# A float32 encoder trunk on one core: the order of VectorE's work in the product blocks, and what is split at the end of a stage

## The chip, the core and the metric

The kernel runs on one core of a Trainium2 chip. The metric is the device time of one execution in microseconds, the median of several runs. TensorE (PE in the profile) multiplies, VectorE (DVE) and ScalarE (ACT) work on elements, GpSimd (POOL) issues some transfers, and SyncE's queue (SP) issues the others.

## The reference

The reference is a two-layer encoder on x of 256 tokens by 1024. Each layer is a feed-forward stage, a mixer and another feed-forward stage, each with a scaled residual and a layer norm behind it:

```python
def swiglu(x, w_in, w_out):
    gu = x @ w_in                              # 1024 x 5632
    g, u = gu[..., :D_FF], gu[..., D_FF:]      # D_FF = 2816
    return (jax.nn.silu(g) * u) @ w_out        # 2816 x 1024

def reference(x, ffn_w_in, ffn_w_out, ln_g, ln_b, ml_w_in, ..., at_w_out):
    for l in range(DEPTH):                     # 2
        x = layer_norm(ALPHA * x + 0.5 * swiglu(x, ffn_w_in[l, 0], ffn_w_out[l, 0]), ln_g[l, 0], ln_b[l, 0])
        y = mlstm_mixer(x, ...) if l == 0 else window_attention(x, ...)
        x = layer_norm(ALPHA * x + y, ln_g[l, 1], ln_b[l, 1])
        x = layer_norm(ALPHA * x + 0.5 * swiglu(x, ffn_w_in[l, 1], ffn_w_out[l, 1]), ln_g[l, 2], ln_b[l, 2])
    return x
```

The mixers are a bidirectional chunkwise mLSTM in layer 0 and a windowed attention with sinks in layer 1. Everything is float32.

## The kernel before

There are six stages: feed-forward, mLSTM, feed-forward, feed-forward, attention, feed-forward. To keep float32 accuracy, each operand of a matmul is split into a high and a low part: ScalarE writes the high part (`w_hi`, `h_hi`, `xT_hi`) and VectorE the difference as the low part (`w_lo`, `h_lo`, `xT_lo`). A product is then three matmuls (`mm3`): high by high, high by low, low by high.

**Weights.** All weights come from HBM as words of 128 partitions by 1024 values (512 KB). The class `Weights` (L155) holds the plan: a list of splits in a fixed order, each of one word. `load` issues a word's transfer on SP when a buffer is free (four for the tag `w_raw`; two for each of the tags `s_raw0` to `s_raw3`). `high` emits the ScalarE part of the next split, `low` the VectorE part, then drops the word's use and loads the next. Split words live in a ring of ten (`RING`). `take` gives the next words to a product, and forces the splits that are still missing; `done` says that words have been used.

**Seven products.** A feed-forward stage computes its first 768 columns of gate and up plainly. The other 2048 go in four blocks of 512 (`SEVENS`), each done by `seven` as a two-by-two block product with seven products in place of eight. Some of its weights are sums of words: VectorE adds one word to another (`tensor_add` in `sum`), or GpSimd issues a transfer that accumulates on top of a word already in SBUF. So the words `b11` of a block are split four times, at four states, and between two of these stands an addition or an accumulating transfer. `after` holds these additions by split, `needs` says which split has to come first. The plan's order differs from the order of use in one thing: the last two splits of a block (`late`) stand behind the first two of the next block; `turn` gives the order of use.

Inside a block the products are, in order, on the PSUM banks qa, qc, qb, qa, qa, qb, qa, with down-projections (`down`, twelve matmuls for each word of w_out) between them: three stand in the middle and one at the end of a full block, two in the last block. Behind each product an `end` function emits its element work on the tile `e` (names v["g0"], v["u0"], v["u1"], v["g1"]). `tr` turns a half of h = silu(g) * u by four TensorE transposes, and `split_evac` writes it as `h_hi` (ScalarE) and `h_lo` (VectorE). In a full block `tr` of v["u0"] stands behind the third down-projection, before the last product; `tr` of v["u1"] stands in the next block, behind its first product.

**The clocks.** While it writes the program, the class `Paced` keeps an estimate of each engine's time: `pe`, `vec`, `act` and `dma`, and of when each tile will be there (`when`, `mark`). In a feed-forward stage each matmul that is written calls `fill` (L278). It emits a split's high part if ScalarE's clock is less than 300 ns (`AHEAD`) ahead of TensorE's and the word is there 1000 ns (`SOON`) before; and, if VectorE's clock allows it, an addition or a low part under the same rule. All other VectorE work is written where its producer is written, and each engine runs its instructions in the written order. A transfer's landing is estimated as 2200 ns (`LANDING`) and 1340 ns (`LOADING`) behind TensorE's clock, that of an accumulating one as 8000 ns (`ADDING`).

**The end of a stage.** Behind the last block `fill` is switched off (`nc.filler = None`, L920), `load_ln` issues two transfers on SP for the layer norm's vectors (L921), and the last six words are taken. `W.done(0)` (L924) then splits as many of the next stage's words as the ring has room for, whether they have landed or not. `tail` (L612) does the last down-projections: first token half 0, both output halves, then token half 1. In between it runs the transposes of the last block (`between`), the residual and the layer norm (`Norm`, L569), and more calls of `W.done`, with numbers of splits from lists at the head of the file.

Of the kernel before, what the change touches and what calls it, by code (L numbers as in the profile page):

```python
# [45 lines left out]
SOON = -1000.0  # L46
LANDING = 2200.0
LOADING = 1340.0
SECOND = 1250.0
ADDING = 8000.0  # L50
# [98 lines left out]
class Weights:  # L149
# [5 lines left out]
    def __init__(self, nc, pool, words, plan, after, turns):  # L155
        self.nc, self.pool, self.words, self.plan, self.after = nc, pool, words, plan, after
        self.raw, self.parts, self.half, self.sums = {}, {}, [], []
        self.made = self.used = self.gone = 0
        self.room = 0
        self.order, self.left = turns, set(range(len(plan)))  # L160
        self.todo = {tag: [i for i, w in enumerate(words) if w["tag"] == tag] for tag in TAGS}
        self.free = {"v_raw": 0, **{tag: 0 for tag in TAGS}, "w_raw": RAW_BUFS}
        self.spool, self.send, self.vbufs = None, 0, 0
        self.uses = [0] * len(words)
# [49 lines left out]
    def split(self, upto):  # L214
        while self.made < min(upto, len(self.plan)):
            self.high()
        while self.half and self.half[0][0] < upto:
            self.low()

    def high(self):  # L220

        nc, i = self.nc, self.made
# [18 lines left out]
        self.made += 1  # L241
        return True

    def low(self):
# [15 lines left out]
        self.sums += [(i, *sum_) for sum_ in self.after.get(i, ())]  # L260
# [3 lines left out]
    def sum(self):  # L264
        nc = self.nc
        _, w, v = self.sums.pop(0)
        t = self.raw[w]
        if isinstance(v, int):
            nc.vector.tensor_add(t, t, self.raw[v])
            self.drop(v)  # L270
            self.load()
        else:
            nc.gpsimd.dma_start(t.rearrange("p (k f) -> p k f", k=self.words[w]["k"]), v, accum_op=OP.add)  # L273
            now = max(nc.vec, nc.pe)
            nc.dma = max(nc.dma, now + LANDING) + SHARE
            nc.mark(t, now + ADDING)

    def fill(self):  # L278

        nc = self.nc  # L280
        while True:
            act, vec = max(nc.act, nc.pe), max(nc.vec, nc.pe)
            if act < nc.pe + AHEAD and len(self.half) < 2 and self.made < min(self.room, len(self.plan)):
                p = self.plan[self.made]
                if (p["word"] in self.raw and nc.when(self.raw[p["word"]]) < act + SOON
                        and not any(p["needs"] == x for x in [h[0] for h in self.half] + [s_[0] for s_ in self.sums])):
                    self.high()
                    continue
            if vec < nc.pe + AHEAD:
                if self.sums and nc.when(*(self.raw[w] for w in self.sums[0][1:] if isinstance(w, int))) < vec + SOON:  # L290
                    self.sum()
                    continue
                if self.half and nc.when(self.half[0][1]) < vec + SOON:
                    self.low()
                    continue
            break

    def take(self, n):
        these = self.order[self.used:self.used + n]
        self.used += n  # L300
        self.split(max(these) + 1)
        return [self.parts[j] for j in these]
# [4 lines left out]
    def done(self, upto=None, most=None, high_only=False):  # L307
# [3 lines left out]
        while self.gone < upto:  # L311
            j = self.order[self.gone]
            self.left.discard(j)
            self.parts.pop(j, None)
            self.gone += 1
        self.room = max(self.room, min(self.left, default=len(self.plan)) + RING)
# [15 lines left out]
def trunk_kernel(ctx: ExitStack, tc: tile.TileContext, x, ffn_w_in, ffn_w_out, ln_g, ln_b, ml_w_in, ml_gate_b,  # L332
# [17 lines left out]
    def split_of(w, scale=None, needs=None):  # L350

        plan.append(dict(word=w, k=words[w]["k"], scale=scale, needs=needs, turn=len(plan)))
# [22 lines left out]
    def seven(w, c0, c1, n, down, late):  # L375
# [6 lines left out]
        first = len(plan)  # L382
        used = iter(range(99))

        def turn(n_):
            for p in plan[-n_:]:
                p["turn"] = first + 0.01 * next(used)

        s1 = [split_of(w_) for w_ in b11]
        turn(2)  # L390
        for j, a in enumerate(at(512, c1)):
            after[s1[j]] = [(b11[j], b12[j]), (b12[j], a)]
        late()
        for a in at(512, c0):
            piece(a, 2)
        turn(2)
        down()
        turn(1)
        s5 = [split_of(w_, None, p) for w_, p in zip(b11, s1)]
        turn(2)  # L400
        for j in range(2):
            after[s5[j]] = [(b11[j], b22[j])]
        full = n < SEVENS - 1
        s6 = [split_of(w_, None, p) for w_, p in zip(b11, s5)]
        turn(2)
        for j, a in enumerate(at(512, c0)):
            after[s6[j]] = [(b11[j], a)]
        down()
        turn(1)
        [split_of(w_, None, p) for w_, p in zip(b12, s1)]  # L410
        turn(2)
        for w_ in b22:
            split_of(w_)
        turn(2)
        if full:
            down()
            turn(1)
        at4 = [next(used) for _ in range(2)]
        if full:
            down()  # L420
            turn(1)

        def last():
            for j in range(2):
                split_of(b11[j], None, s6[j])
                plan[-1]["turn"] = first + 0.01 * at4[j]
        return last

    ends = {}
    for j, (kind, l, i, _) in enumerate(stages):  # L430
        if kind == "ffn":
# [13 lines left out]
            late = lambda: None  # L445
            for g in range(SEVENS):
                c0 = 768 + 512 * g
                late = seven(wi, c0, F + c0, g, lambda: down(1), late)
            late()
# [33 lines left out]
    W = Weights(nc, wpool, words, plan, after, [j for _, j in sorted((p['turn'], j) for j, p in enumerate(plan))])  # L483
# [52 lines left out]
    def split_evac(dst, src, scale=None, high=None):  # L536
        if scale is None:
            (high or nc.scalar.copy)(dst[0], src)
            nc.vector.tensor_sub(dst[1], src, dst[0].bitcast(F32))
# [20 lines left out]
    def load_ln(room, l, n):  # L560
        t = []
        for name, w in (("g", ln_g), ("b", ln_b)):
            a = room("ln_" + name)
            src = w[l, n]
            nc.sync.dma_start(a, bass.AP(tensor=src.tensor, offset=src.offset, ap=[[0, 128], [1, D]]))
# [46 lines left out]
    def tail(y, h, todo, first, norm, last, turn_at, between=None):  # L612
# [37 lines left out]
        W.done(most=TD[bound[0]])  # L650
        return lambda: emit_x(1, last)
# [5 lines left out]
    def ffn(l, i, n, pending, last):  # L657
        with ExitStack() as ph:
# [18 lines left out]
            def tr(hB, t, h):  # L677
# [3 lines left out]
                split_evac(pair(hB, A, A, tok(t)), p)  # L681
# [50 lines left out]
            def x_sum(name, a, op, b):  # L732
# [4 lines left out]
                split_evac(xs[name], f)  # L737
# [90 lines left out]

            def seven(full, before):
# [11 lines left out]
                def end2():  # L841
                    nc.vector.tensor_add(v["g0"], v["g0"], qc)
# [4 lines left out]
                def end6():  # L847
                    v["u0"] = copied(qa, "e2")
                    nc.scalar.activation(v["g0"], v["g0"], AF.Silu)

                def end3():
                    nc.vector.tensor_sub(v["u0"], qb, v["u0"])
                    nc.vector.tensor_mul(v["u0"], v["g0"], v["u0"])

                def end7():
                    nc.vector.tensor_sub(v["u1"], v["u1"], qa)
# [18 lines left out]
                if full:  # L875
                    down(1)
                    tr(hB, 0, v["u0"])
# [3 lines left out]
                return lambda: tr(hB, 1, v["u1"])  # L881
# [26 lines left out]
            def turn():  # L908
# [4 lines left out]
                split_evac(hp, p)  # L913
# [4 lines left out]
            if start:  # L918
                small_loads()
            nc.filler = None  # L920
            gb = load_ln(lambda name: pool.tile([128, D], F32, name=name, tag=TAGS[1], bufs=S_RAW), l, n)  # L921
# [552 lines left out]
```

## Time and profile before

| | |
|---|---|
| median of 3 runs | 948.33 us (946.0 to 948.74) |
| profiled execution, its own time | 948.53 us |
| its span, first to last instruction | 946.8 us |
| granted TensorE clock, mean over the span | 0.984 |
| TensorE busy | 918.3 us (97%) |
| VectorE busy | 810.6 us (86%) |
| ScalarE busy | 569.5 us (60%) |
| read from HBM | 206.65 MB, 219 GB/s over the span |

Nearly all compute instructions carry line L140, where a helper records each operation; so they are told apart by engine and tile: `pw` and `py` are PSUM banks (products, and down-projections or output projections), `w_hi` and `w_lo` the split weights, `s_raw` words of the blocks with sums, `w_raw` the other words, `e` the element work of a block. In a row such as `PE pw L140 <- DVE e L140: 7.7, 8, 2.3` the engine on the left waited for the one on the right, 7.7 us in all, 8 times, 2.3 us at most. In rows of the windows the columns are the stretch and its length, then for each engine the busy us and the number of instructions, the granted TensorE clock, the share of the DMA engines and GB/s. In a chain the columns are start, us and what.

### The profile page before, as it was taken

How to read it: one execution, taken by the hardware profiler on the slowest of the kernel's cores; microseconds unless marked ns; L12 is line 12 of the kernel's file. 1: busy time of each engine (PE TensorE's matmuls, PEld its weight loads, DVE VectorE, ACT ScalarE, POOL GpSimd, SP SyncE). 2: the span in 40 equal slices, each digit the busy share in tenths (PEclk: the TensorE clock that was granted, in tenths of full speed). 3: DMA queues.
4: the chain of work that ended last, by engine and by line, in shares of the span. 5: the costliest groups of instructions: out<-in, count | busy, mean ns of one | idle time of the engine just before them, and what ended most of it. 6: DMA issues, size and time to landing. Idle time of an engine off the chain costs nothing.

```text
span 946.8 us, 12553 instructions
## 1 busy us (share of the span) xinstructions
PE 918.3 (97%) x4459; PEld 763.5 (81%) x4459; DVE 810.6 (86%) x969; ACT 569.5 (60%) x793; POOL 155.5 (16%) x194
## 2 busy tenths in 40 slices
PE   9998999999999999999989999997999999999997
PEld 7786887889988888788878878886888888788885
DVE  5798998897699789999787999987868887989986
ACT  5575674645764566775535766764459564676670
POOL 0011122022321011211011111210345301212110
PEclk9998999999999999999989999999999999999999
DMA  8988997754625979987649799867343379889951
GB/s 283 354 202 272 275 283 165 239 173 151 225 95 178 335 186 321 252 251 204 218 146 356 178 278 310 252 156 235 121 156 120 104 246 287 233 224 274 290 135 45
DMA packets 100703, 208.53 MB, mean 220 GB/s; under 512 B 6904, under 2 KB 21264, under 8 KB 100640
## 3 DMA queue, kind: packets, MB, share of 16 engines
q1 hardware_dynamic: 82368, 173.04, 52.0%
q0 software_dynamic: 17696, 33.65, 20.6%
q10 hardware_dynamic: 576, 1.05, 0.3%
q8 instruction: 35, 0.57, 0.3%
q14 instruction: 28, 0.23, 0.1%
HBM read 206.65 MB, written 1.05 MB: 219 GB/s over the span
## 4 chain that ended last, share of the span: by engine, by line
PE 60%; DVE 18%; DMA 13%; issue 5%; ACT 3%; POOL 0%; SPq 0%; DVEq 0%; ACTq 0%; POOLq 0%
PE pw L140 39%; PE py L140 21%; DVE w_lo L140 11%; DMA s_raw<-in_ffn_w_in_dram 7%; DMA w_raw<-in_ffn_w_in_dram 3%; DVE e L140 2%; ACT w_hi L140 2%; DMA w_raw<-in_ffn_w_out_dram 1%; DVE s_raw L140 1%; DMA w_raw<-in_at_w_in_dram 1%; DVE h L140 1%; DVE h_lo L140 1%; POOL hrs L1111 0%; DVE x L140 0%; DVE S_lo L140 0%
## 5 line engine op out<-in xcount | busy, mean ns | idle before, releaser
L140 DVE TENSOR_TENSOR w_lo<-w_raw,w_hi 128x1024 fp32r<-128x1024 f32 (+1 forms) x213 | 254.1, 1219 | 29.6 <-ACT w_hi L140 27.6
L140 ACT CAST w_hi<-w_raw 128x1024 fp32r<-128x1024 f32 (+1 forms) x213 | 217.7, 1048 | 86.3 <-DMA w_raw<-in_ffn_w_in_dram 26.3
L140 DVE TENSOR_TENSOR w_lo<-s_raw,w_hi 128x1024 fp32r<-128x1024 f32 x192 | 228.8, 1219 | 11.5 <-ACT w_hi L140 11.4
L140 ACT CAST w_hi<-s_raw 128x1024 fp32r<-128x1024 f32 x192 | 193.4, 1052 | 59.8 <-DVE s_raw L140 55.0
L140 PE MATMUL pw<-w_hi,xT_hi 128*128 128x512 f32 x480 | 192.4, 402 | 0.0
L140 PE MATMUL pw<-w_lo,xT_hi 128*128 128x512 f32 x480 | 188.9, 395 | 3.5 <-DVE w_lo L140 3.5
L140 PE MATMUL pw<-w_hi,xT_lo 128*128 128x512 f32 x480 | 188.9, 395 | 0.0
L273 POOL DMA_DIRECT2D s_raw<-in_ffn_w_in_dram x64 | 77.4, 1209 | 503.6 <-DVE w_lo L140 190.8
L140 PE MATMUL py<-w_hi,h_hi 128*128 128x512 f32 x349 | 139.2, 399 | 3.8 <-ACT h_hi L140 3.8
L140 PE MATMUL py<-w_hi,h_lo 128*128 128x512 f32 x349 | 138.6, 397 | 3.9 <-DVE h_lo L140 3.9
L140 PE MATMUL py<-w_lo,h_hi 128*128 128x512 f32 x349 | 137.8, 395 | 0.2 <-DVE w_lo L140 0.2
L140 PEld LDWEIGHTS pw<-w_lo,xT_hi 128*128 128x128 f32 x480 | 91.5, 191 | 22.8 <-DVE w_lo L140 5.1
L140 PEld LDWEIGHTS pw<-w_hi,xT_lo 128*128 128x128 f32 x480 | 91.3, 190 | 19.9 <-DVE xT_lo L140 0.2
L140 PEld LDWEIGHTS pw<-w_hi,xT_hi 128*128 128x128 f32 x480 | 91.4, 191 | 17.6 <-issue 0.2
L140 PE MATMUL pw<-w_lo,S_hi 128*128 128x512 f32 x256 | 99.7, 389 | 0.0
L140 PE MATMUL pw<-w_hi,S_lo 128*128 128x512 f32 x256 | 99.6, 389 | 0.0
L140 PE MATMUL pw<-w_hi,S_hi 128*128 128x512 f32 x256 | 99.6, 389 | 0.0
L140 DVE TENSOR_TENSOR s_raw<-s_raw,s_raw 128x1024 f32<-128x1024 f32 x64 | 78.4, 1225 | 9.5 <-DMA s_raw<-in_ffn_w_in_dram 7.7
L140 PEld LDWEIGHTS py<-w_hi,h_lo 128*128 128x128 f32 x349 | 66.7, 191 | 19.4 <-DVE h_lo L140 5.2
L140 PEld LDWEIGHTS py<-w_hi,h_hi 128*128 128x128 f32 x349 | 66.9, 192 | 18.6 <-ACT h_hi L140 4.7
L140 PEld LDWEIGHTS py<-w_lo,h_hi 128*128 128x128 f32 x349 | 66.8, 191 | 14.4 <-DVE w_lo L140 0.6
L140 ACT CAST h_hi<-pw 128x512 fp32r<-128x512 f32 x44 | 25.7, 587 | 60.0 <-PE pw L140 60.0
(205 smaller groups left out, 1156.3 us busy)
## 6 DMA issues: line engine op xcount, KB each, us to landing
s_raw<-in_ffn_w_in_dram SPq DMA_DIRECT2D x96, 512.0 KB, 8.1
w_raw<-in_ffn_w_out_dram SPq DMA_DIRECT2D x88, 512.0 KB, 6.5
w_raw<-in_ffn_w_in_dram SPq DMA_DIRECT2D x64, 512.0 KB, 5.5
s_raw<-in_ffn_w_in_dram POOLq DMA_DIRECT2D x64, 512.0 KB, 7.6
w_raw<-in_ml_w_in_dram SPq DMA_DIRECT2D x24, 512.0 KB, 4.7
w_raw<-in_ffn_w_in_dram SPq DMA_DIRECT2D x32, 256.0 KB, 3.5
w_raw<-in_at_w_in_dram SPq DMA_DIRECT2D x12, 512.0 KB, 4.8
w_raw<-in_ml_w_out_dram SPq DMA_DIRECT2D x8, 512.0 KB, 4.3
```

The costliest lines, as they stand in the source:

```text
L140: r = f(out, *args, **kw)
L273: nc.gpsimd.dma_start(t.rearrange("p (k f) -> p k f", k=self.words[w]["k"]), v, accum_op=OP.add)
```

## The change

The change does five things.

- VectorE work that reads what TensorE or ScalarE has just made (`split_evac` with `wait=True`, and the sums and products of the `end` functions) is handed to `when_ready`. In a feed-forward stage it is kept in a list, and `fill` emits it once the clocks have its operands there; `flush` emits what is left ahead of each `down`, of transposes that need it, and of the stage's end. Low parts are emitted 300 ns behind their high part in place of 1000, and an added word counts as there 700 ns (`NEAR`) before VectorE's clock.
- The plan is in order of use; `late` and `turn` are gone. `next` looks at up to six (`LOOK`) splits that are not yet made and takes the first whose word is there. Accumulating transfers are issued as soon as the split or addition in front of them is emitted, and count as landed after 7000 ns.
- In full blocks `tr` of v["u0"] moves behind the last product, as it stood in the last block before.
- `load_ln` moves from behind the last block to behind its first product, and is entered in the clocks.
- From the end of the last block to the end of `tail` (`landed`), `done` splits a word of the next stage only if the clocks have had it landed for 1000 ns; what is not split is counted in `owed` and tried again at later calls, of which there is now one behind each step of the tail's first part. At the end of `tail` the rest of `owed` is dropped.

```diff
+NEAR = -700.0
+LOOK = 6
-ADDING = 8000.0
+ADDING = 7000.0
...
+    def next(self, act):
+        nc = self.nc
+        free = RING - (len(self.made) - self.gone)
+        i = self.first_left()
+        for n in range(min(LOOK, free)):
+            while i in self.made:
+                i += 1
+            if i >= len(self.plan):
+                break
+            p = self.plan[i]
+            if (p["word"] in self.raw and nc.when(self.raw[p["word"]]) < act + SOON
+                    and (p["needs"] is None or p["needs"] in self.made)
+                    and not any(p["needs"] == x for x in [h[0] for h in self.half] + [s_[0] for s_ in self.sums])):
+                return i
+            i += 1
+        return None
...
+    def when_ready(self, f, *ins):
+        if self.nc.filler is None:
+            f()
+        else:
+            self.later.append((f, ins))
+
+    def flush(self):
+        while self.later:
+            self.later.pop(0)[0]()
...
     def fill(self):
...
+            if act < nc.pe + AHEAD and len(self.half) < 2:
+                i = self.next(act)
+                if i is not None:
+                    self.high(i)
                     continue
+            if self.later and nc.when(*self.later[0][1]) < vec:
+                self.later.pop(0)[0]()
+                continue
             if vec < nc.pe + AHEAD:
-                if self.sums and nc.when(*(self.raw[w] for w in self.sums[0][1:] if isinstance(w, int))) < vec + SOON:
+                add = self.sums and nc.when(*(self.raw[w] for w in self.sums[0][1:])) < vec + SOON
+                if add and self.sums[0][0] != self.fresh:
                     self.sum()
                     continue
-                if self.half and nc.when(self.half[0][1]) < vec + SOON:
+                if self.half and nc.when(self.half[0][1]) < vec - 300.0:
                     self.low()
                     continue
+                if add:
+                    self.sum()
+                    continue
             break
...
     def done(self, upto=None, most=None, high_only=False):
...
-        end = min(self.room if most is None else min(self.room, self.made + most), len(self.plan))
-        while self.made < end and self.high():
-            pass
+        room = RING - (len(self.made) - self.gone)
+        most = room if most is None else most
+        if self.landed:
+            self.owed += most
+            most = min(self.owed, max(most, 1))
+        n = 0
+        while n < min(most, room) and self.first_left() < len(self.plan):
+            w = self.plan[self.left]["word"]
+            if self.landed and w in self.raw and self.nc.when(self.raw[w]) > max(self.nc.act, self.nc.pe) + SOON:
+                break
+            if not self.high(self.left):
+                break
+            n += 1
+        if self.landed:
+            self.owed -= n
...
-            nc.sync.dma_start(a, bass.AP(tensor=src.tensor, offset=src.offset, ap=[[0, 128], [1, D]]))
+            nc.load(a, bass.AP(tensor=src.tensor, offset=src.offset, ap=[[0, 128], [1, D]]))
...
                 one(0, o, n)
+                if W.landed:
+                    W.done(0, 0)
...
         W.done(most=TD[bound[0]])
+        W.owed, W.landed = 0, False
...
             def seven(full, before):
...
                 def end2():
-                    nc.vector.tensor_add(v["g0"], v["g0"], qc)
+                    W.when_ready(lambda: nc.vector.tensor_add(v["g0"], v["g0"], qc), qc)
...
                 def end4():
                     v["g1"] = temp("g1")
                     nc.scalar.activation(v["g1"], qa, AF.Silu)
-                    if not full:
-                        tr(hB, 0, v["u0"])
-                    nc.vector.tensor_mul(v["u1"], v["g1"], v["u1"])
+                    W.flush()
+                    tr(hB, 0, v["u0"])
+                    W.when_ready(lambda: nc.vector.tensor_mul(v["u1"], v["g1"], v["u1"]), v["g1"])
...
                 before()
+                if not full:
+                    gb.extend(load_ln(lambda name: pool.tile([128, D], F32, name=name, tag=TAGS[1], bufs=S_RAW), l, n))
                 product(qc, of(4, 0), True, end2)
...
                 if full:
                     down(1)
-                    tr(hB, 0, v["u0"])
                 product(qa, of(4, 1), False, end4)
...
+            W.flush()
             nc.filler = None
-            gb = load_ln(lambda name: pool.tile([128, D], F32, name=name, tag=TAGS[1], bufs=S_RAW), l, n)
+            W.landed = True
```

More of the change, by code (lines that the diff above doesn't have):

```diff
@@ L163, in __init__ @@
         self.spool, self.send, self.vbufs = None, 0, 0
+        self.later, self.fresh, self.owed, self.landed = [], None, 0, False
         self.uses = [0] * len(words)
@@ L214, in split, with first_left, high @@
     def split(self, upto):
-        while self.made < min(upto, len(self.plan)):
-            self.high()
-        while self.half and self.half[0][0] < upto:
+        for i in range(min(upto, len(self.plan))):
+            if i not in self.made:
+                self.high(i)
+        while any(h[0] < upto for h in self.half):
             self.low()
-    def high(self):
-        nc, i = self.nc, self.made
+    def first_left(self):
+        while self.left in self.made:
+            self.left += 1
+        return self.left
+    def next(self, act):
[14 more added lines that the diff above has]
+        return None
+    def high(self, i):
+        nc = self.nc
         p = self.plan[i]
@@ L240, in high @@
         self.half.append((i, hi))
[L241 removed]
+        self.made.add(i)
         return True
@@ L259, in low @@
         self.parts[i] = (hi.rearrange("p (k f) -> p k f", k=k), lo.rearrange("p (k f) -> p k f", k=k))
-        self.sums += [(i, *sum_) for sum_ in self.after.get(i, ())]
+        self.fresh = i
+        sums = [(i, *sum_) for sum_ in self.after.get(i, ())]
+        while sums and not isinstance(sums[0][2], int):
+            self.transfer(*sums.pop(0)[1:])
+        self.sums += sums
         self.drop(p["word"])
@@ L298, in take @@
     def take(self, n):
-        these = self.order[self.used:self.used + n]
+        i = self.used
         self.used += n
-        self.split(max(these) + 1)
-        return [self.parts[j] for j in these]
+        self.split(self.used)
+        return [self.parts[j] for j in range(i, i + n)]
     def take_rows(self, n):
@@ L310, in done @@
         upto = self.used if upto is None else upto
[L311 to L316, printed above, removed]
+        for j in [j for j in self.parts if j < upto]:
+            del self.parts[j]
+        self.gone = max(self.gone, upto)
         if self.nc.filler is not None:
```

130 lines of the change are left out of this document (60 added, 70 removed).

## The prediction

> **What bounds the kernel now.** I read the page first, then TensorE's own waits, then the chain that ended last in order of time, and last the stages' windows and the timelines of single queues where TensorE stood still.
>
> ```profile
> span 946.8 us, 12553 instructions
> PE 918.3 (97%) x4459; PEld 763.5 (81%) x4459; DVE 810.6 (86%) x969; ACT 569.5 (60%) x793; POOL 155.5 (16%) x194
> PE 60%; DVE 18%; DMA 13%; issue 5%; ACT 3%; POOL 0%; SPq 0%; DVEq 0%; ACTq 0%; POOLq 0%
> ```
>
> TensorE is busy for 97% of the span. The change removes no matmul, so all it can win is time in which TensorE stands still or runs slowly. The waits name that time, by engine and tile:
>
> ```profile
> PE pw L140 <- DVE e L140: 7.7, 8, 2.3
> PE py L140 <- DVE h_lo L140: 3.9, 2, 2.0
> PE py L140 <- ACT h_hi L140: 3.8, 2, 3.1
> PE pw L140 <- DVE w_lo L140: 3.5, 2, 3.2
> ```
>
> The columns are total us, times, and the longest. Four kinds make up nearly all of it, 18.9 us. The chain gives start, us and count; here are ordinary pieces and the pieces right behind a wait:
>
> ```profile
> 348.90 2.72 PE py L140 x12
> 400.16 3.38 PE pw L140 x16
> ...
> 78.77 4.93 PE pw L140 x11
> 144.20 4.97 PE pw L140 x16
> 476.58 10.44 PE py L140 x36
> 662.42 9.75 PE py L140 x36
> 827.41 4.99 PE pw L140 x16
> ```
>
> Twelve matmuls take 2.72 us, 0.227 each. Sixteen instructions (4 transposes, 12 matmuls) take 3.38 us at 400.16, and 4.97 and 4.99 at 144.20 and 827.41: behind a wait TensorE runs slowly for a while. The granted clock says the same:
>
> ```profile
> core 0: us, PE busy (x) PEld busy (x) DVE busy (x) ACT busy (x) POOL busy (x), PEclk, DMA share, GB/s
> 73.00:85.00 12.00, 7.89 (x27) 5.89 (x26) 9.68 (x12) 5.63 (x7) 2.41 (x2) 0.72 1.08 316
> 368.00:400.00 32.00, 31.06 (x140) 25.48 (x140) 29.73 (x30) 21.46 (x25) 4.81 (x4) 1.00 0.94 268
> 432.00:470.00 38.00, 38.00 (x175) 31.42 (x174) 33.61 (x34) 24.42 (x29) 2.41 (x2) 1.00 0.65 178
> 584.00:615.00 31.00, 30.98 (x140) 25.36 (x140) 29.57 (x30) 21.57 (x25) 4.81 (x4) 1.00 0.93 271
> 654.00:668.00 14.00, 9.04 (x29) 6.59 (x28) 8.97 (x12) 2.57 (x3) 1.46 (x1) 0.76 0.57 205
> 822.00:834.00 12.00, 9.69 (x38) 7.74 (x37) 10.25 (x12) 4.25 (x6) 1.60 (x2) 0.86 1.08 318
> ```
>
> It is 0.72, 0.76 and 0.86 around three of the waits and 1.00 where there is none to speak of. So each longer wait is paid for twice. The rows 368:400 and 584:615 are about one full seven-product block each: VectorE is busy 29.73 of 32 and 29.57 of 31 us. It has only some 1.4 to 2.3 us a block to spare.
>
> **The change, part by part.** The sum is made against the profiled execution's 948.53 us (span 946.8 and 1.7 around it), 0.2 over the median of the runs shown.
>
> *Transposes of u0 moved (term A).* In the three full blocks of each feed-forward stage, the transposes that read `e` (tr of v["u0"]) stood right behind a down-projection; now they stand behind the block's last product, twelve matmuls later. All 8 waits on DVE `e` that the trace lists end at four such transposes, as here:
>
> ```profile
> 73.42 0.39 PE L140 MATMUL py<-w_hi,h_lo 128*128 128x512 f32 x1
> 74.73 0.63 PE L140 MATMUL pw<-ident,e 128*128 128x128 f32 x4 [0.93 <-DVE e L140]
> ```
>
> The py in front is the down-projection. The move gives VectorE 2.72 us more, and the longest wait is 2.3. What it issues moves with it: four transposes, a ScalarE h_hi and a VectorE h_lo, on ScalarE past one Silu that waits for the same product. These h are first read by the next block's downs, a down, two products and a transpose later (over 8 us by the 2.72 row), so that costs nothing. Worth at most 7.7 us, and the slow running behind two of these waits, 4.97 - 3.38 and 4.99 - 3.38, 3.2 us: 10.9. VectorE's spare time is small, so some of what no longer shows at the transposes will show at a w_lo; I take 9.3.
>
> The Trainium skill (TensorE: Matmul & The Clock Gate, What's actually happening) says the clock falls after an idle window of about 3.4 us. Here a wait of 2.3 us was followed by the slow piece at 827.41, so the trace doesn't agree with that as a least length. By the page the two shorter waits would have cost no clock, term A would be 7.7 at most, and the forecast some 2.7 us higher; I go by the rows.
>
> *VectorE's order (term B).* The operations that read PSUM or a fresh ScalarE result (low parts, u0, u1, g0) no longer enter VectorE's queue at the end of a product but when the clocks say the operand is there; a forced emission before each down and transpose keeps them from being too late. A low part needs only 0.3 us behind ScalarE instead of 1 us, an addition hands its word on 0.8 us sooner, accumulating transfers are put on POOL's queue at once (their start is set by VectorE's last read, so they gain little), and up to six splits are looked at instead of one. The last two splits of a block, once written behind the next block's first two, now come ahead of them if their word is there. The counts of splits, additions and transfers stay as they are. What TensorE can win is the w_lo wait and its slow piece at 78.77: 3.5 + (4.93 - 11 x 0.227 = 2.4) = 5.9. That wait is on one of those last splits, behind two of the next block's lows and two additions on VectorE, which now may stand behind it. But VectorE hardly idles there, and the u0 move brings TensorE to this spot sooner, so I take half, 3.0.
>
> The price is unknown: with less margin VectorE and ScalarE can stand at the head of their queues before the operand is there.
>
> ```profile
> DVE w_lo L140 <- ACT w_hi L140: 39.6, 30, 4.4
> 384.25 7.85 DMA s_raw<-in_ffn_w_in_dram
> s_raw<-in_ffn_w_in_dram POOLq DMA_DIRECT2D x64, 512.0 KB, 7.6
> w_raw<-in_at_w_in_dram SPq DMA_DIRECT2D x12, 512.0 KB, 4.8
> ln_g<-in_ln_g_dram SPq DMA_DIRECT2D x6, 512.0 KB, 5.9
> ln_b<-in_ln_b_dram SPq DMA_DIRECT2D x6, 512.0 KB, 6.8
> ```
>
> VectorE already waits 39.6 us for w_hi, in 30 places. An accumulating transfer lands 7.6 us behind its issue in the median, and the clocks now allow its split 7 + 1 us behind the VectorE operation that frees it, so about half of these splits could be issued a little early; ScalarE, busy 21.5 of 32 us in a block, can stand that. Less waiting on VectorE is possible too, and would be a gain, but TensorE can win no more than its own waits. Bounds: 0, if the spare 1.4 us a block absorbs it, to 12 x 1 us if each of the 12 full blocks loses 1 us more than it has. The nearest row is the quiet 584:615 one, where these hand-overs hide; I take 1.5 us of cost.
>
> *LN vectors earlier, next stage's words only once landed (term C).* At two ends of feed-forward stages ScalarE stands at a word of the next stage:
>
> ```profile
> 647.86 0.45 SPq L565 DMA_DIRECT2D ln_g<-in_ln_g_dram  x1
> 648.40 0.38 SPq L565 DMA_DIRECT2D ln_b<-in_ln_b_dram  x1
> 649.83 8.24 DMA w_raw<-in_at_w_in_dram
> 658.15 1.04 ACT L140 CAST w_hi<-w_raw 128x1024 fp32r<-128x1024 f32 x1 [4.61 <-DMA w_raw<-in_at_w_in_dram]
> 659.10 0.58 ACT L140 CAST h_hi<-pw 128x512 fp32r<-128x512 f32 x1
> ...
> ACT w_hi L140 <- DMA w_raw<-in_ffn_w_in_dram: 3.3, 1, 3.3
> 466.32 5.91 DMA w_raw<-in_ffn_w_in_dram
> ```
>
> Two LN loads of 512 KB go out just ahead of the word, which lands after 8.24 us (4.8 is the median of its kind). ScalarE waits 4.61 us for it, with the h_hi that TensorE needs queued behind; VectorE then does that word's w_lo and a normalisation step before h_lo. That is the h_hi and h_lo waits above: 3.8 + 3.9 = 7.7, and the slow pieces, 10.44 - 3 x 2.72 = 2.3 and 9.75 - 3 x 2.72 = 1.6: 11.6. After the change the LN loads are issued in the last block's first product, some 20 us before, and a split is emitted only if the clocks have had its word for 1 us; otherwise it stays owed, and is tried again behind each of the twelve steps that follow. h_hi then comes first. What is late next is at most one word, for about 1 us, because the clocks' landing (about 3.5 us, and the 1 us of margin) is near the real one. I take four fifths, 9.3. The other ends show no wait in this trace and stay.
>
> On SP's queue the two loads move ahead of the last block's remaining down-projection words. They wait for two s_raw0 buffers, whose last low parts TensorE has already used by then, so nothing behind them is held. They bring 1 MB into the last block, where DMA share is 0.65 and TensorE busy 38.00 of 38 us: 512 KB take 5.9 to 6.8 us to land, and what is in flight beside them can be late by the 8.24 - 4.8 = 3.4 us seen above. That block's accumulations have until its last product, so I charge nothing; if that cover is gone, up to 4 x 2 us (3.4 less VectorE's 1.4 spare, in four stages). The Trainium skill (DMA: Bandwidth & Descriptors, Issuing engines are not separate DMA queues) says transfers of all issuers interleave on the same 16 engines, which speaks against this move: LN loads on SP can delay POOL's accumulations. The 8.24 us row agrees as far as one queue goes; no row here shows it across the two.
>
> Sum: 9.3 + 3.0 + 9.3 - 1.5 = 20.1 us, and 948.5 - 20.1 gives 928.4.
>
> **The rivals.** (1) VectorE is the bound in the blocks, and time only moves: the u0 waits return at w_lo, half of A and none of B is won, and words not landed by the clocks are owed and dropped at the stage's end, so half of C comes back as w_lo waits at the next stage's start. 948.5 - 5.5 - 5.8 + 1.5 = 938.7. For it: VectorE 29.57 of 31 us. Against it: block 584:615 runs with TensorE busy 30.98 of 31. I see 936 to 945 for it, with 0.17.
>
> (2) Slower: VectorE taken too early. With 0.3 us of margin the in-order VectorE stands at lows whose w_hi is late, whenever ScalarE is behind its clock, for instance at a split whose accumulation lands after 8 us. A full block has 18 lows; at 0.25 us of waiting each it loses 4.5 us, 3 more than the 1.4 it has, and 12 blocks make 37 us against the 20 won: 965. It decides from about 0.17 us a low (12 x (18 x 0.17 - 1.4) = 20). For it: 39.6 us of such waits now. Against it: in the blocks they are rare, since VectorE has other work queued. With smaller waits 952 to 965; chance 0.16.
>
> (3) The reordering does nothing, because VectorE's clock is nearly always ahead of TensorE's, and deferred work is emitted at the next matmul as before; then B is 0 and the cost too: 948.5 - 18.6 = 929.9. That is within the forecast.
>
> **How the numbers follow.** Forecast, 918 to 936: 0.61. Rival 1, 936 to 945: 0.17. No change, when gains and rival 2 balance: 0.06. Slower: 0.16. A measurement of this kernel tells about 0.3%, 2.8 us, from no change; so faster 0.78, same 0.06, slower 0.16. The range leaves out the slower cases and little else: its low end, 917, is all three terms, 10.9 + 5.9 + 11.6 = 28.4, with 3 us of small waits the list doesn't reach; its high end, 946, is rival 1 with the last block's 8 us charged.
>
> **What would show it.** Right: TensorE's waits on DVE `e` under 2 us in all; h_hi and h_lo waits under 2; the LN issues some 20 us ahead of the stage's end; ScalarE's w_hi waits on DMA at both ends under 1 us; granted clock near 1.00 at what were 140, 472, 658 and 825 us. B is wrong if TensorE's w_lo waits grow over 6 us. Wrong altogether: VectorE waiting for w_hi well over 40 us and blocks longer than 32 us, or w_lo waits at the starts of the stages.

## The result, and the profile after

The changed kernel takes 935.52 us in the median of 4 runs (930.02 to 936.08), the kernel before 948.54 beside it. The ratio is 0.9864, with a 95% interval of 0.9833 to 0.9896: 13 us faster (1.4%), where 20 were forecast. The profiled execution took 935.22 us, 13.3 less than the one before.

The head of the page and TensorE's waits after:

```profile
span 933.5 us, 12591 instructions
PE 913.5 (98%) x4459; PEld 759.4 (81%) x4459; DVE 804.1 (86%) x969; ACT 568.6 (61%) x793; POOL 156.1 (17%) x194
...
PE py L142 <- ACT h_hi L142: 3.1, 3, 1.7
PE pw L142 <- ACT e L142: 2.5, 2, 2.2
PE py L142 <- DVE h_lo L142: 2.4, 5, 0.5
PE py L142 <- DVE w_lo L142: 1.7, 2, 1.5
...
PE pw L142 <- DVE e L142: 0.9, 2, 0.6
PE pw L142 <- DVE w_lo L142: 0.2, 1, 0.2
```

The waits for VectorE's `e` fell from 7.7 us to 0.9, those of products for w_lo from 3.5 to 0.2. New are a wait for ScalarE's `e`, 2.5 us, and one of down-projections for w_lo, 1.7 us (0.4 before), and there are still 5.5 us for h_hi and h_lo. But these are in other places. The windows show it: first a full block, then the two ends that stood still before, then three new places.

```profile
570.00:601.00 31.00, 31.00 (x142) 25.69 (x141) 28.92 (x29) 20.50 (x25) 4.81 (x4) 1.00 0.91 253
445.00:475.00 30.00, 30.00 (x134) 23.98 (x134) 29.09 (x32) 18.06 (x22) 3.90 (x3) 1.00 0.72 212
632.00:660.00 28.00, 28.00 (x133) 23.25 (x132) 26.24 (x32) 15.08 (x18) 1.46 (x1) 1.00 0.58 179
...
800.00:812.00 12.00, 9.85 (x36) 7.65 (x35) 6.64 (x7) 7.22 (x9) 0.00 (x0) 0.86 1.02 358
505.00:520.00 15.00, 13.58 (x53) 10.23 (x52) 12.56 (x16) 7.85 (x11) 1.20 (x1) 0.89 0.93 279
160.00:175.00 15.00, 13.32 (x53) 10.23 (x52) 12.69 (x15) 9.02 (x10) 1.25 (x1) 0.89 0.71 199
```

The block and both ends are now full at a clock of 1.00. The new places are a block of the last feed-forward stage (800), the start of the third (505), and the end of the first (160). In each TensorE waits and then runs at a lowered clock. (The second and the last stage start with like waits, 1.1 and 2.0 us in all, but at a clock of 1.00.) Two timelines show on what TensorE waits. The first is the block: ScalarE, then TensorE.

```profile
804.84 1.04 ACT L142 CAST w_hi<-s_raw 128x1024 fp32r<-128x1024 f32 x1 [4.38 <-DMA s_raw<-in_ffn_w_in_dram]
805.79 0.58 ACT L142 COPY e<-pw 128x512 f32<-128x512 f32 x1
...
803.88 0.39 PE L142 MATMUL py<-w_hi,h_lo 128*128 128x512 f32 x1
806.42 0.68 PE L142 MATMUL pw<-w_hi,S_hi 128*128 128x512 f32 x1 [2.15 <-ACT e L142]
```

ScalarE stands 4.38 us at a word whose transfer hasn't landed (whether it was a plain load or an accumulating transfer the trace leaves open). The copy of `e`, which frees the bank that TensorE needs next, is queued behind. The second is the start of a stage: SP's issues, then ScalarE.

```profile
485.63 1.06 SPq L108 DMA_DIRECT2D w_raw<-in_ffn_w_out_dram  x2
486.74 7.31 SPq L108 DMA_DIRECT2D s_raw<-in_ffn_w_in_dram  x8
494.67 1.90 SPq L108 DMA_DIRECT2D w_raw<-in_ffn_w_in_dram  x2
497.37 1.70 SPq L108 DMA_DIRECT2D w_raw<-in_ffn_w_out_dram  x2
...
505.54 1.05 ACT L142 CAST w_hi<-w_raw 128x1024 fp32r<-128x1024 f32 x1 [5.18 <-DMA w_raw<-in_ffn_w_in_dram]
...
508.80 1.05 ACT L142 CAST w_hi<-w_raw 128x1024 fp32r<-128x1024 f32 x1 [0.86 <-DMA w_raw<-in_ffn_w_out_dram]
509.76 0.61 ACT L142 CAST S_hi<-S 128x512 fp32r<-128x512 f32 x1
...
512.86 0.62 ACT L142 CAST S_hi<-S 128x512 fp32r<-128x512 f32 x1 [1.54 <-DVE S L142]
513.39 0.58 ACT L142 CAST h_hi<-pw 128x512 fp32r<-128x512 f32 x1
```

Fourteen loads go out in 14 us. ScalarE stands 5.18 us at one word of w_in, briefly at the next, and 0.86 us at a word of w_out. S_hi (the high part of an operand for a block's products) comes behind, VectorE's next S after it, and h_hi behind that; TensorE waits for h_hi. The long wait itself isn't new. At the same place of the kernel before ScalarE stood too, but S_hi came right behind the words of w_in:

```profile
514.68 1.05 ACT L140 CAST w_hi<-w_raw 128x1024 fp32r<-128x1024 f32 x1 [4.59 <-DMA w_raw<-in_ffn_w_in_dram]
...
516.99 0.61 ACT L140 CAST S_hi<-S 128x512 fp32r<-128x512 f32 x1
```

New is the split of a word of w_out ahead of S_hi. The second and the last stage start in the same way: waits of 4.39 and 5.81 us for a word of w_in (4.14 and 5.71 before), and then, as did not happen before, of 1.76 and 1.09 us for a word of w_out ahead of S_hi. Summed over the run, ScalarE's waits for transfers and VectorE's for w_hi are:

```profile
DVE w_lo L142 <- ACT w_hi L142: 53.0, 40, 4.2
ACT w_hi L142 <- DMA s_raw<-in_ffn_w_in_dram: 34.9, 19, 5.4
ACT w_hi L142 <- DMA w_raw<-in_ffn_w_in_dram: 34.2, 20, 5.8
```

In the kernel before, ScalarE waited less for both:

```profile
ACT w_hi L140 <- DMA w_raw<-in_ffn_w_in_dram: 26.3, 12, 5.7
...
ACT w_hi L140 <- DMA s_raw<-in_ffn_w_in_dram: 4.5, 3, 1.7
```

So 16 of the 19 waits for s_raw came with the change. Most of them cost nothing, as a run below shows (landing_5500).

### The profile page after: what moved, and what is told of

The parts are those of the page before. It is cut to its first block, busy times and chain, and to the rows that moved or that the text cites. A ratio compares the mean times of both kernels' runs of the same rounds, so it can differ in the third digit from the quotient of the medians.

```text
span 933.5 us, 12591 instructions
## 1 busy us (share of the span) xinstructions
PE 913.5 (98%) x4459; PEld 759.4 (81%) x4459; DVE 804.1 (86%) x969; ACT 568.6 (61%) x793; POOL 156.1 (17%) x194
## 5 line engine op out<-in xcount | busy, mean ns | idle before, releaser
L142 ACT CAST w_hi<-w_raw 128x1024 fp32r<-128x1024 f32 (+1 forms) x213 | 216.7, 1047 | 80.9 <-DMA w_raw<-in_ffn_w_in_dram 34.2
L142 PE MATMUL pw<-w_hi,xT_hi 128*128 128x512 f32 x480 | 190.1, 397 | 0.9 <-DVE e L142 0.9
L142 PE MATMUL pw<-w_hi,xT_lo 128*128 128x512 f32 x480 | 187.0, 391 | 0.0
L142 PE MATMUL pw<-w_lo,xT_hi 128*128 128x512 f32 x480 | 186.6, 390 | 0.2 <-DVE w_lo L142 0.2
L142 DVE TENSOR_TENSOR s_raw<-s_raw,s_raw 128x1024 f32<-128x1024 f32 x64 | 76.4, 1220 | 0.0
L142 ACT COPY e<-pw 128x512 f32<-128x512 f32 x48 | 28.0, 584 | 56.2 <-PE pw L142 56.1
```

Source lines behind the costliest of these rows:

```text
L142: r = f(out, *args, **kw)
```

## The experiments

All times are medians, with the ratio to the kernel before on the same chip and its 95% interval. The kernel before itself took 947.4, 948.36 and 949.07 us in the three groups of runs, so where two kernels of different groups are compared, the ratios count for more than the difference of the medians.

| kernel | us | ratio |
|---|---|---|
| u0_back | 942.5 | 0.9943 (0.9922 to 0.9965) |
| no_defer | 933.75 | 0.9854 (0.9834 to 0.9873) |
| end_as_before | 935.71 | 0.9873 (0.9842 to 0.9905) |
| adding_9500 | 944.06 | 0.9965 (0.9946 to 0.9984) |
| only_u0 | 945.14 | 0.9961 (0.9945 to 0.9977) |
| only_ends | 938.29 | 0.9890 (0.9870 to 0.9910) |
| look_1 | 961.07 | 1.0138 (1.0102 to 1.0173) |
| landing_4000 | 926.93 | 0.9791 (0.9767 to 0.9816) |
| ends_before_l4000 | 929.68 | 0.9799 (0.9775 to 0.9823) |
| before_l4000 | 943.68 | 0.9945 (0.9928 to 0.9963) |
| landing_5500 | 922.71 | 0.9726 (0.9706 to 0.9746) |
| l4000_no_defer | 938.85 | 0.9894 (0.9877 to 0.9911) |

**The transposes of u0 put back.**

```diff
-                    tr(hB, 0, v["u0"])
+                    if not full:
+                        tr(hB, 0, v["u0"])
...
                 if full:
                     down(1)
+                    W.flush()
+                    tr(hB, 0, v["u0"])
```

> The changed kernel with one thing undone: in full blocks the transposes of u0 stand again behind the third down-projection. Theory (the move is what took TensorE's waits for e away): these waits come back to 6 us or more in some 8 places, with two or three slow pieces behind them, and the time is 942 to 946 us. Rival (VectorE's order by the clocks had cured them by itself, the move is idle): waits for e stay under 2.5 us and the time is 933 to 938.

```profile
PE pw L142 <- DVE e L142: 11.2, 9, 3.1
```

The waits for `e` are back and larger than before the change, and the time is 7 us above the changed kernel. So the move took them away, and VectorE's order by the clocks doesn't.

**The move alone, on the kernel before.**

```diff
-                    if not full:
-                        tr(hB, 0, v["u0"])
+                    tr(hB, 0, v["u0"])
...
                 if full:
                     down(1)
-                    tr(hB, 0, v["u0"])
```

> The kernel before with one thing of the change: in full blocks the transposes of u0 stand behind the last product. Theory (the move alone takes away the waits for e, 7.7 us and 3.2 of slow running): 937 to 941 us, no wait for e over 0.5 us. Rival (VectorE is the bound in the blocks, the time only moves to w_lo): TensorE's waits for w_lo grow to 8 us or more and the time is 943 to 948.

Both were half right. The waits for `e` went (0.6 us are left), but only 0.4% of time with them. TensorE's other waits:

```profile
PE py L140 <- DVE h_lo L140: 5.4, 3, 2.0
PE pw L140 <- DVE w_lo L140: 5.1, 2, 4.4
PE py L140 <- ACT h_hi L140: 5.1, 4, 2.8
```

w_lo grew by 1.6 us, h_hi and h_lo by 2.8: a third end, that of the first feed-forward stage, now stands still too (a wait of 2.0 us for h_lo, 1.2 for h_hi, with ScalarE waiting 3.7 us there for a word of the mLSTM stage). Together with smaller ones, TensorE's listed waits sum to 20.9 us here and 21.2 before: in this execution (942.47 us) no waiting was won, only slow running. A TensorE that comes sooner finds the next late thing.

**The ends of the feed-forward stages undone.**

```diff
-                if not full:
-                    gb.extend(load_ln(...))
...
             nc.filler = None
-            W.landed = True
+            gb.extend(load_ln(...))
+            W.landed = False
```

> The changed kernel with the end of a feed-forward stage undone: the two LN loads behind the last block, and the next stage's words split whether landed or not. Theory (this part won what the h_hi and h_lo waits at two ends cost, 7.7 us of waits and 3.9 of slow running, and gave some 3 us back at the first stage's end, where words of w_out now land late): 942 to 947 us, with ScalarE waiting 3 to 5 us for a word of the next stage at the ends of the second and third feed-forward stages. Rival (the new order in the blocks had moved those waits away by itself): 933 to 938.

The rival holds: 935.71 us, as the changed kernel (935.52), with runs from 931.0 to 940.7. A sixth run, which took 946.07 us, is in neither the median nor the ratio. The profile is of that one; it has no wait for h_hi or h_lo over 0.3 us at the two ends, but waits of 4.43 and 5.61 us for w_lo at the starts of the third and the last stage. With a later landing estimate (LANDING 4000, below) the same undoing gives a quieter run:

> The changed kernel with LANDING 4000, and with the end of a feed-forward stage as before (LN loads behind the last block, no waiting for landed words). Theory (what the later landing wins, it wins at the stages' starts and in the blocks; with the new block order the end edits are nearly idle): 925 to 931 us. Rival (it wins at the ends, where only words landed by the clocks are split): 934 or more, with ScalarE waiting 3 us or more for a word ahead of h_hi at an end.

929.68 us against 926.93, the intervals overlapping: the theory holds. At the end that stood still before, SP's issues and ScalarE in this run:

```profile
450.86 9.11 SPq L108 DMA_DIRECT2D w_raw<-in_ffn_w_in_dram  x4
460.31 0.34 SPq L108 DMA_DIRECT2D ln_g<-in_ln_g_dram  x1
...
464.60 1.05 ACT L142 CAST w_hi<-w_raw 128x1024 fp32r<-128x1024 f32 x1 [1.44 <-DMA w_raw<-in_ffn_w_in_dram]
466.57 0.59 ACT L142 CAST h_hi<-pw 128x512 fp32r<-128x512 f32 x1 [0.92 <-PE pw L142]
```

The LN loads are behind the block again and words are split whether landed or not; still h_hi waits for nothing but TensorE. The next stage's first words go out from 450.86 on, almost 16 us before this h_hi and 9.5 before the LN loads (at LANDING 2200, in end_as_before, 15 and 9). In the kernel before the like row is

```profile
459.15 5.10 SPq L106 DMA_DIRECT2D w_raw<-in_ffn_w_in_dram  x3
```

5 us ahead of its LN loads at 464.30. Words are loaded when a buffer comes free, so the rest of the change has the last words of the stage split sooner; which of its parts does that these runs don't separate (only_u0 shows that it isn't the move of u0).

**The ends alone, on the kernel before.** LN loads, `landed`, `owed` and the calls in `tail` as in the change, with `done` of the kernel before:

```diff
...
+        while self.made < end:
+            w = self.plan[self.made]["word"]
+            if self.landed and w in self.raw and self.nc.when(self.raw[w]) > max(self.nc.act, self.nc.pe) + SOON:
+                break
+            if not self.high():
+                break
...
```

> The kernel before with the end of a feed-forward stage as changed: LN loads in the last block, the next stage's words split only once landed by the clocks; order and lookahead in the blocks as before. Theory (this cures the ends by itself, as the new block order does too, which is why undoing it cost little): the h_hi and h_lo waits fall under 2 us and the time is 935 to 940 us. Rival (only the new block order, which has the words of the stage's end loaded earlier, cures them): 944 us or more, with ScalarE still waiting 3 us or more for a word ahead of h_hi.

938.29 us, 10 less than before, and no wait for h_hi is left in TensorE's list. So the end edits cure the ends, and the rest of the change does it too: each is enough, and they don't add up. `e` rose here, from 7.7 to 10.5 us.

**VectorE's deferred work emitted at once.**

```diff
-        if self.nc.filler is None:
+        if True:
             f()
```

> The changed kernel with when_ready emitting at once, so VectorE's low parts and block sums enter its queue where they are written, as before; the lookahead, the 300 ns margin and all else stay. Theory (with a nearly saturated VectorE its clock is ahead of TensorE's, so deferred work is emitted at the next matmul anyway): 933 to 939 us, VectorE's waits for TensorE at e around 7 us as before. Rival (the order by the clocks carries the gain in the blocks): TensorE's waits for e and w_lo grow by 5 us or more, 941 or more.

933.75 us, not above the changed kernel: the theory holds in time. The rival's waits came all the same: those of products for w_lo rose from 0.2 to 5.7 us, in 10 places, and those for `e` from 0.9 to 3.5. But the waits for h_hi, h_lo, ScalarE's `e` and down-projections' w_lo fell from 9.7 to 2.2. With LANDING 4000 this turns over:

> The changed kernel with LANDING 4000 and when_ready emitting at once. Theory (the deferred order of VectorE carries nothing, as its undoing alone showed): 925 to 930 us. Rival (with TensorE waiting less VectorE is nearer to its bound, and its order counts): 932 or more, waits for e or w_lo 4 us above those with LANDING 4000 alone.

938.85 us against 926.93 (ratios 0.9894 and 0.9791, so 10 to 12 us). TensorE's waits:

```profile
PE pw L142 <- DVE w_lo L142: 9.3, 10, 1.4
PE pw L142 <- DVE e L142: 3.2, 3, 2.5
```

The rival holds. Waits for w_lo and `e` rise here by 11.3 us (from 1.2), as they rose by 8.1 at LANDING 2200; but with LANDING 4000 the four other kinds, which had fallen by 7.5 there, were down to 4.3 already, and little was left to win against it. Why emitting at once shortened those waits the runs don't show.

**A later landing of accumulating transfers.**

```diff
-ADDING = 7000.0
+ADDING = 9500.0
```

> The changed kernel with one number: an accumulating transfer counts as landed after 9500 ns in place of 7000. Theory (ScalarE is put on such words before they have landed, 34.9 us of waiting in 19 places, and what stands behind it makes TensorE wait for e, about 3.4 us of waits and one slow stretch): ScalarE's waits for s_raw transfers fall under 10 us, and the time is 928 to 933 us. Rival (a later split makes w_lo late for the block's last product): TensorE's waits for w_lo grow to 5 us or more and the time is 937 or more.

My theory fell. ScalarE's waits for s_raw did fall, to 13.4 us, and no wait for `e` is left, but the time rose to 944.06:

```profile
PE pw L142 <- DVE w_lo L142: 9.3, 5, 2.3
PE py L142 <- ACT h_hi L142: 8.3, 2, 4.9
```

Four waits of 2.2 to 2.3 us for w_lo stand one in each feed-forward stage, as the rival said; the two for h_hi stand at stages' starts, and why they grew this run doesn't tell.

**One split of lookahead.**

```diff
-LOOK = 6
+LOOK = 1
```

> The changed kernel with a lookahead of one split in place of six, so splits are made strictly in order of use. Theory (with the lookahead the first block's sums and their accumulating transfers start amid the burst of loads at a stage's start and make w_out's first words land late there; in order they start later): the waits at the first down-projections of the second, third and last feed-forward stages, some 9 us with the slow running in this trace, fall under 3 us; but a block's last splits hold up all behind them, so w_lo or e waits in the blocks rise by 3 us or more; 930 to 940 us. Rival (the starts wait because ScalarE is put on words too early, with or without lookahead): the waits at the starts stay at 5 us or more.

961.07 us, slower than the kernel before, and outside the theory's range.

```profile
PE pw L142 <- ACT e L142: 12.1, 10, 2.1
...
PE py L142 <- DVE w_lo L142: 5.2, 3, 3.7
...
ACT w_hi L142 <- DMA s_raw<-in_ffn_w_in_dram: 50.3, 15, 4.9
```

ScalarE's copies of `e` are late in ten places, behind splits that wait for transfers; and the starts of the third and the last feed-forward stage still wait (w_lo, 3.7 and 1.2 us), as the rival said. So the lookahead isn't all that makes the starts wait, and it carries the plan in order of use: without it the new plan loses 25 us.

**A later landing of loads.**

```diff
-LANDING = 2200.0
+LANDING = 4000.0
```

> The changed kernel with one number: a load counts as landed 1800 ns later (LANDING 4000 in place of 2200). Theory (at the stages' starts the words land 6 to 13 us behind their issue, the clocks say 3.5 to 6, and ScalarE stands at them ahead of S_hi and h_hi): ScalarE's waits for w_raw transfers fall by 10 us or more, the waits at the starts by half, 928 to 933 us. Rival (TensorE needs these very words, so it waits whatever stands ahead of h_hi): 934 to 940, TensorE waiting for w_lo in place of h_hi.

926.93 us, 8.6 below the changed kernel (7 by the ratios), and a little below the theory's range: the theory holds. No wait for h_hi is left in TensorE's list, the waits for h_lo are 0.7 us, and the third stage's start is nearly full:

```profile
500.00:520.00 20.00, 19.64 (x90) 15.69 (x89) 17.21 (x21) 9.76 (x13) 2.42 (x2) 1.00 0.90 285
...
ACT w_hi L142 <- DMA w_raw<-in_ffn_w_in_dram: 24.9, 13, 5.7
```

ScalarE's waits for w_raw words of in_ffn_w_in fell from 34.2 to 24.9, those for words of in_ffn_w_out from 7.7 to 2.0. At the stages' starts ScalarE's long wait for a word of w_in stays (4.44, 4.71 and 5.70 us); what changed is that the next w_raw word, by the order of loads that of w_out, is split behind S_hi and no longer ahead of it. It wins this without the end edits too (ends_before_l4000 above).

> The kernel before with LANDING 4000 in place of 2200, nothing else. Theory (the landing estimate matters because the change lets the clocks choose among splits and hold back words; with the plan's fixed order it decides little): 945 to 950 us, the waits for e, h_hi, h_lo and w_lo much as before. Rival (the low estimate was a fault by itself, apart from the change): 942 or less.

943.68 us, 5 below the kernel before: between the two. So with both kernels at LANDING 4000 the change is worth some 15 us by the ratios (0.9945 and 0.9791; 17 by the medians) in place of 13. `e` fell from 7.7 to 2.0, w_lo and h_lo rose to 4.7 and 6.2.

> The changed kernel with LANDING 5500. Theory (words land 4 to 13 us behind their issue; with 4000 most splits come behind the landing, more margin makes splits late): 927 to 934 us, TensorE's w_lo waits above those with 4000 (2.7 us). Rival (the estimate is still too low in the bursts): under 926 us.

922.71 us, the fastest of all, 2.7% below the kernel before and 12.8 us below the change. The rival holds for the time: 4000 was still too low. A kernel before with 5500 was not run, so how much of this the change owes to itself stays open. TensorE's longest wait but the kernel's first, the start of the third feed-forward stage, and two waits that did not shrink:

```profile
PE pw L142 <- ACT e L142: 1.5, 2, 0.9
...
500.00:520.00 20.00, 20.00 (x94) 16.59 (x93) 19.61 (x24) 13.93 (x20) 2.58 (x3) 1.00 0.79 237
...
DVE w_lo L142 <- ACT w_hi L142: 56.6, 47, 3.7
...
ACT w_hi L142 <- DMA s_raw<-in_ffn_w_in_dram: 35.3, 22, 4.1
```

The stage's start is full. What is left to TensorE is the first wait of the kernel, 1.7 us, and waits under 1 us. ScalarE's waits for s_raw are as long as in the changed kernel (34.9): here they cost TensorE next to nothing.

## Why the prediction was right, and what it mis-sized

The sign and the range (917 to 946) held; the gain was 13.0 us against 20.1, so the time lies at the very edge of the forecast, 918 to 936. That it lies so near is partly luck: the three terms came out 5.7 us larger than taken (27.3 against 21.6), the cost 12.5 us larger. By its steps, on one profiled execution of each kernel:

- **Term A** (u0 moved, 9.3 of 10.9). The waits for `e` fell by 6.8 us, and where the two slow pieces stood the clock is 1.00 (windows 140 to 155 and 815 to 830): 10.0. u0_back shows that the move did it. What the text missed is that alone it pays only 3.7 us (only_u0).
- **Term B** (w_lo, 3.0 of 5.9). The wait fell by 3.3 us, and its slow piece went (clock 1.00 from 70 to 85): 5.7. Half was too careful. Which edit did it the runs don't separate; the wait at this place stays away without the deferral (no_defer) and without the lookahead (look_1).
- **Term C** (ends, 9.3 of 11.6). Both ends are full: 11.6. The price was right, the cause one of two: only_ends cures the ends, and the rest of the change cures them as well. That a split waits for its word did not hold throughout: at the second stage's end ScalarE stood 2.69 us at a word of the next stage (at 463.05), where under 1 was named as a sign; it cost nothing, since h_hi had time to spare. The LN loads did hold up accumulations in two of the last blocks (below), but none that TensorE waited for.
- **The cost** (1.5). This is the step that failed. The three terms gave 10.0 + 5.7 + 11.6 = 27.3, and the executions differ by 13.3, so 14.0 us of new waits and slow running came. The rows above name 3.1 + 2.5 + 2.4 + 1.7 = 9.7 as waits, of which 0.4 were there before: 9.3. The other 4.7 is slow running, and the three windows at 0.86 and 0.89 hold nearly all of it. I had looked for the price on VectorE, standing at lows. It begins on ScalarE. "About half of these splits could be issued a little early; ScalarE ... can stand that" counted ScalarE's free time and not what is queued behind the waiting split: it holds for most of these waits, and not at 804.84. "The clocks' landing (about 3.5 us, and the 1 us of margin) is near the real one" was read at the ends; at the starts, where 14 loads queue, a word issued at 494.67 was split at 505.54. The kernel before stood at such words as well; what the change's order of splits added is a word of w_out split ahead of S_hi. With LANDING at 4000 and 5500 the time is 8.6 and 12.8 us lower, most of the 14.0, though not all of that is the change's own: the kernel before wins 5 by LANDING 4000 too, so 2 to 4 us of this gain is the change's own.

**The rivals.** Of rival 1, time did move, but to ScalarE's work and hardly to w_lo: one such wait, 1.49 us at the last stage's start, is what the prediction had named as a sign of being wrong. Of rival 2, VectorE's waits for w_hi did rise, from 39.6 to 53.0 us, past the 40 that I had named as a sign of a loss; they are 56.6 in the kernel of 922.71 us, so such waits are no price by themselves. Rival 3 looked right in time for the changed kernel (no_defer), though not in its waits, and is wrong where TensorE waits less (l4000_no_defer).

The clock behaved as the rows of before had it: behind the wait of 2.15 us that ends at 806.42 it is 0.86 over the window; there matmuls start 0.43 us apart for 3.5 us, in place of 0.23. The Trainium skill (TensorE: Matmul & The Clock Gate, What's actually happening) has it fall after about 3.4 us idle; these traces show it after less. Nor does the length of a wait decide alone: 0.85 and 0.47 us at the third stage's start are followed by slow running, 1.49 and 0.47 at the last stage's start are not. The same Trainium skill's rule that all issuers' transfers interleave (DMA: Bandwidth & Descriptors, Issuing engines are not separate DMA queues) fits the LN loads, which land later in the last block, beside other loads and accumulating transfers, than behind it: 7.3 and 8.1 us in the median, 5.9 and 6.8 before. In the last blocks of the third and the last feed-forward stage GpSimd's accumulating transfers start, by the profile, only when ln_b has landed:

```profile
POOL s_raw L308 <- DMA ln_b<-in_ln_b_dram: 25.3, 2, 12.7
```

TensorE has no wait over 0.3 us behind them. Whether the LN loads slowed transfers beside them no run here shows apart. At the first stage's end a word of w_out kept ScalarE waiting 1.49 us ahead of h_hi; that the LN loads made it late is argued, not shown.

## What to carry to other kernels

Where an order is written by estimated clocks, compare the estimates with the trace's landings first, in bursts too: an estimate that is too low turns into a wait at the head of an in-order queue, and the price is what stands behind it, not the waiting engine's own time. Here one number for the landing, on top of the change, was worth as much as the whole change (12.8 against 13.0 us). And a wait that is taken off the bottleneck engine alone brings it sooner to the next one: 10.9 us of waits and slow running, taken away alone, paid 3.7.

## What was not expected

Two edits that each cured the same two ends (the end edits alone are worth 10 us, and beside the rest of the change next to nothing), so that undoing either one costs little and hides its worth. And the deferral of VectorE's work, worth nothing at one landing estimate and 10 to 12 us at another.
